# Where an adaLN modulation vector is summed while TensorE feeds sixteen state-space scans: on GpSimd, or in quarters of TensorE's columns

## The chip, the cores and the metric

The kernel runs on one core of a Trainium2 chip. The metric is the device time of one execution in microseconds (us). Its engines are TensorE (PE in the profile; its weight loads are PEld), VectorE (DVE), ScalarE (ACT), GpSimd (POOL) and SyncE (SP), whose queue issues nearly all transfers. Each engine works through its own instructions in order and waits for the others by semaphores.

## The reference, cut to what matters

One layer of a hybrid diffusion backbone, for 2048 tokens of 1024 channels and 256 context tokens, all in float32:

```python
sh1, sc1, gt1, sh2, sc2, gt2 = adaln(c, w_ada, b_ada)       # silu(c) @ w_ada + b_ada, six vectors of 1024
h = rms_norm(x, g_pre_mix) * (1 + sc1) + sh1                # the context likewise
u, xr, gr = split(h @ w_in, [512, 1024])                    # 512 channels each
y_s5  = s5_glu(D * u + S5 scans of u in both directions)    # 32 groups of 16 channels, 64 complex states each
y_lru = (RG-LRU of conv(xr) in both directions) * gelu(gr)
x = x + gt1 * rms_norm(concat(y_s5, y_lru) @ w_out, g_post_mix)
x = x + gt2 * rms_norm(swiglu(rms_norm(x, g_pre_ffn) * (1 + sc2) + sh2), g_post_ffn)
```

The change concerns the vectors gt1, sh2 and sc2 (numbers i = 2, 3, 4 of `w_ada`'s six blocks of 1024 columns). Each is a product of a row of 1024 numbers with a 1024x1024 block of `w_ada`. The first two vectors are made earlier, the last one (gt2) later; neither way is changed.

## The kernel before, in words

Products are in float32 precision on TensorE: a factor is split into a high and a low part (L59 on ScalarE rounds, L62 on VectorE takes the difference), and three matmuls (L70 to L72) make one product. A product of the input projection is one tile of 128 output channels for one block of 512 tokens: 8 slices of the 1024 inputs, three matmuls each, 24 in all. There are 12 tiles of channels: 0 to 3 are u for the S5 scans, 4 to 7 are the LRU input (stored in `XRD`), 8 to 11 the gate (stored in `GGD`). There are five token blocks, the context (n = 0, 256 tokens, no gate) and four of the latents.

**`u_pass`** makes tiles 0 to 5 (0 to 3 and the LRU input's first two) for all five blocks, normalising and transposing the tokens as it goes. **`rest_pass`** makes what is left, block 4 first, whose tokens still lie in SBUF, then blocks 0, 1, 2, 3, whose normalised tokens it loads again from `HD` (tile `hty`) and splits again into tiles `ht` and `wx`. It is a generator: each `next` issues one product ("a fill product" below) and returns what it is said to cost, 5.4 or 2.8.

**`s5_main`** handles 16 pairs of S5 groups. A half pair is one direction of one pair: TensorE makes the scan's inputs `pv` (a state group, L774: four matmuls with 64 output columns each), VectorE turns them, scans them and turns them back (L780 to L797, into `sf`). After the second direction of a pair TensorE reads out the pair before (a readout, L805 and L812: ten matmuls into the PSUM banks `py0` and `py1`), ScalarE applies GELU (`yt`, L814), and eight transfers store it in `YD`.

**`mix`** sets TensorE's order by hand for this stage. First it issues `AHEAD` fill products. Then `run` steps `s5_main`, adds `S5_FILL` to what is owed at each half pair, and issues fill products until what they are said to cost has paid it. At every half pair it also steps **`ada_s5`** once. What is left of the fills stands at the stage's end; then the LRU stage begins, whose convolution needs `XRD`.

`ada_s5` makes gt1, sh2 and sc2. `ada_sum` loads 128 rows of `w_ada` at a time (eight loads of 512 KB for a vector, through the two buffers `alw`); GpSimd multiplies each row by its number of silu(c) (L1128, L1130) and adds it to an accumulator `g` or `alacc` (L1131). What remains is a sum over the 128 partitions: `ada_row` takes it by a matmul with ones and spreads it over all partitions (L1143), adds a bias and multiplies by a gain on VectorE (L1144, L1145); `ada_col` takes it as columns, by eight matmuls with one column of ones (L1152). Both write into the readout's bank `py0`.

Of the kernel before, what the change touches and what calls it, by code (L numbers as in the profile page):

```python
# [9 lines left out]
F32 = mybir.dt.float32  # L10
F32R = mybir.dt.float32r
I32 = mybir.dt.int32
AF = mybir.ActivationFunctionType
ALU = mybir.AluOpType
MUL, ADD, SUB = ALU.mult, ALU.add, ALU.subtract
# [3 lines left out]
D = 1024  # L19
KT = 8  # L20
# [25 lines left out]
class Hybrid:  # L46
# [100 lines left out]
        self.ffn()  # L147


    AHEAD = 2  # L150
    S5_FILL, CONV_FILL, DECAY_FILL, GATES_FILL = 3.9, 0.1, 2.0, (0, 2, 2, 2)
    VW = 5
    XB = 5
    NPRE = 3
# [29 lines left out]
    def mix(self):  # L184


        def run(gen, fill, each=None):
            owed = 0.0
            for want in gen:
                if each:  # L190
                    next(each, None)
                owed += want
                while owed > 0:
                    owed -= next(fill, 1e9)

        aes, bes, self.wes = ExitStack(), ExitStack(), ExitStack()
        lru = self.lru(aes, bes)

        def first():
            yield from self.rest  # L200
            self.ies.close()

        with ExitStack() as es:
            ada = self.ada_s5(es)
            fill = first()
            for _ in range(self.AHEAD):
                next(fill)

            with self.tc.manual_schedule(engines={self.nc.tensor.engine}):
                run(self.s5_main(es), fill, ada)  # L210
            for g in (ada, fill):
                for _ in g:
                    pass
            next(lru)

        def rest():
            with ExitStack() as es:
                yield from self.glu(es)
            with ExitStack() as es:
                yield from self.out_s5(es)  # L220

        fill = rest()
        self.mm = (run, lru, fill, aes, bes)
# [122 lines left out]
    def u_pass(self, es):  # L346

        nc, A = self.nc, self.A
# [3 lines left out]
        def load(n):  # L352
            if n == 0:
                xt = [whole(8 + i) for i in range(2)]
                src = A["ctx"][0].rearrange("(j t) d -> t j d", t=T)
                for t in range(T):
                    nc.sync.dma_start(xt[t // 4][32 * (t % 4):32 * (t % 4) + 32, :], src[t])
                return [(xt[i], i * 128) for i in range(2)]
            tiles = []
            src = A["x"][0].rearrange("(b p t) d -> b p t d", b=2, t=T)  # L360
            for b in range(2):
                for i in range(2):
                    xt = xp.tile([128, D], F32, name="xt")
                    nc.sync.dma_start(xt, src[b, :, 2 * n - 2 + i, :])
                    tiles.append((xt, i * 256 + b * 128))
            return tiles

        def norm(tiles, junk):
            nt = len(tiles)
            ss = sp.tile([128, 4], F32, name="ss")  # L370
            rs = sp.tile([128, 4], F32, name="rs")
            for i, (x, _) in enumerate(tiles):
                self.square(junk, x, ss[:, i:i + 1])
            self.rstd(sp, rs[:, :nt], ss[:, :nt], nt, f"u{nt}")
            for i, (x, _) in enumerate(tiles):
                nc.scalar.activation(x, x, AF.Copy, scale=rs[:, i:i + 1])
# [47 lines left out]
        ws = self.load_w_in(0, self.wip, lambda: next(stages))  # L424
# [10 lines left out]
        for n in range(5):  # L435
            nxt, nh = None, []
            if n < 4:
                nxt = load(n + 1)
                norm(nxt, xp.tile([128, D], mybir.dt.bfloat16, name="junk", bufs=1))


            def after(i):
                if nxt and i in (22, 26, 30, 34, 40, 41, 42, 43):
                    turn(n + 1, nxt, nh, (len(nh),))

            for m in range(6):
                if (n, m) == (4, 2):

                    place = [(self.ht(40 + 2 * i), self.ht(41 + 2 * i)) for i in range(2)]
                    self.wrest = self.load_w_in(768, None, raw, place)  # L450
                product(n, m, hts, after)
                yield 5.2
            hts = nh or hts
        self.hts = hts
        self.wrest += self.load_w_in(1024, self.wip, raw)
        xes.close()
        es.close()
# [377 lines left out]
    def rest_pass(self, es):  # L835

        nc = self.nc
        st = self.pool(es, "ist", 2)
        ps = self.pool(es, "ips", 2, space=PSUM)
        MORE = 4  # L840
        places = cycle([lambda i=i: self.wx(i) for i in range(MORE)] + [lambda i=i: self.ht(i) for i in range(32, 40)])

        def fetch(n, k):
            ntok = 512 if n else CTX
            ht = next(places)()
            y = st.tile([128, 512], F32, name="hty", bufs=4)
            nc.sync.dma_start(y[:, :ntok], self.HD[n][k][:, :ntok])
            self.split(ht[:, 0, :ntok], ht[:, 1, :ntok], y[:, :ntok])
            return ht


        hts = self.hts
        for n, after in ((4, 0), (0, 1), (1, 2), (2, 3), (3, None)):
            ntok = 512 if n else CTX
            nxt = []

            def more(upto):
                if after is not None:
                    nxt.extend(fetch(after, k) for k in range(len(nxt), upto))

            for i in range(6 if n else 2):
                more(min(MORE, i + 1 if n else 2 * i + 2))
                pu = ps.tile([128, 512], F32, name="pu")
                wh, wl = self.wrest[i]
                for k in range(KT):
                    self.mm3(pu[:, :ntok], wh[:, k, :], wl[:, k, :], hts[k][:, 0, :ntok], hts[k][:, 1, :ntok],
                             k == 0, k == KT - 1)
                self.end_rest(n, i + 2, pu, st.tile([128, 512], F32, name="iev"))
                yield 5.4 if n else 2.8
            more(KT)  # L870
            hts = nxt
# [248 lines left out]
    def ada_sum(self, i, acc, tile):  # L1120

        nc, A = self.nc, self.A
        for k in range(KT):
# [7 lines left out]
                nc.gpsimd.tensor_tensor(acc, acc, w, op=ADD)  # L1131
            yield

    def ada_row(self, g, i, gi, rows, bank):

        nc = self.nc
        gain, bias = rows(), rows()
        nc.sync.dma_start(gain, self.A["norm_gains"][0, gi:gi + 1, :].to_broadcast([128, D]))
        nc.sync.dma_start(bias, self.A["b_ada"][:, i * D:(i + 1) * D].to_broadcast([128, D]))
        for h in range(2):  # L1140
            cs = slice(h * 512, (h + 1) * 512)
            pa = bank()
            nc.tensor.matmul(pa, self.ones, g[:, cs], start=True, stop=True)  # L1143
            nc.vector.tensor_tensor(g[:, cs], bias[:, cs], pa, op=ADD)  # L1144
            nc.vector.tensor_tensor(g[:, cs], gain[:, cs], g[:, cs], op=MUL)  # L1145

    def ada_col(self, i, acc, bank):

# [11 lines left out]
            v.scalar_tensor_tensor(self.A2, self.A2, 1.0, self.colsA[:, C_G + 16:C_G + 24], op0=ADD, op1=MUL)  # L1160

    def ada_s5(self, es):
        wp = self.pool(es, "alw", 2, side="right")
        tile = lambda: wp.tile([128, D], F32, name="alw")
        bank = lambda: self.psy.tile([128, 512], F32, name="py0")
        yield from self.ada_sum(2, self.g1, tile)
        for i in (3, 4):
            acc = wp.tile([128, D], F32, name="alacc", bufs=1)
            for k, _ in enumerate(self.ada_sum(i, acc, tile)):
                if k == 2 and i == 3:  # L1170
                    self.ada_row(self.g1, 2, 1, tile, bank)
                yield
            yield
            self.ada_col(i, acc, bank)

# [413 lines left out]
```

## Time and profile before

| | |
|---|---|
| median of 3 runs | 2322.15 us (2320.1 to 2322.33) |
| the profiled execution | 2329.66 us, of which the profile's span is 2327.9 us |
| PE busy | 2101.6 us (90%) |
| DVE busy | 1714.1 us (74%) |
| ACT busy | 994.3 us (43%) |
| POOL busy | 808.7 us (35%) |
| DMA | 403.29 MB, 173 GB/s over the span |

The stages follow one another: setup and `u_pass` to about 285 us, the S5 scans with the fill products to 566 us, then the LRU and the gated output of S5 to about 840 us, then the FFN. A row of the profile names the line, the engine, the operation, the tile written and the tiles read, how often it occurs, its time, and in brackets how long the engine sat idle before it and what it waited for. The matmuls of float32 operands that aren't split show as two records each. Every time of the profile is that of one execution.

### The profile page before, as it was taken

What the parts mean: (1) busy time and instruction counts of PE and PEld (TensorE: products, weight loads), DVE (VectorE), ACT (ScalarE), POOL (GpSimd) and SP (SyncE); (2) the same over time, 40 slices, a digit from 0 to 9 for tenths busy, and PEclk for the clock granted to TensorE, in tenths of its full rate; (3) what the DMA queues carried; (4) which work ended last, traced back from release to release, by engine and by line L of the source; (5) the groups of instructions that cost most, each with busy time, mean ns of one, the idle gap of its engine ahead of it and who ended that gap; (6) DMA issues with size and microseconds to landing.
All of it is one profiled execution on the core that took longest, in us unless ns stands there. A gap on an engine that the chain in (4) does not pass through costs nothing. (4 is left out here: it accounts for less than half of the span.)

```text
span 2327.9 us, 27391 instructions
## 1 busy us (share of the span) xinstructions
PE 2101.6 (90%) x9460; PEld 1662.1 (71%) x9460; DVE 1714.1 (74%) x2243; ACT 994.3 (43%) x1561; POOL 808.7 (35%) x478
## 2 busy tenths in 40 slices
PE   6599998897674899879999999999999999999987
PEld 1477865575564677658888887788888878888866
DVE  6985458999998748956777878977787763534768
ACT  4688412112777626763333334333333333232424
POOL 1431420440000003343335545656565511400682
PEclk8799999898886899889999999999999999999999
DMA  9577756765233377863443334544444375634663
GB/s 261 171 243 255 232 149 211 212 206 171 71 122 115 127 236 251 285 222 108 146 136 127 109 100 141 176 139 160 143 156 145 136 262 172 214 100 157 226 219 121
DMA packets 311627, 403.29 MB, mean 173 GB/s; under 512 B 60176, under 2 KB 222528, under 8 KB 309952
## 3 DMA queue, kind: packets, MB, share of 16 engines
q1 hardware_dynamic: 311360, 401.50, 53.2%
q8 instruction: 75, 1.23, 0.2%
q14 instruction: 64, 0.52, 0.1%
q0 software_dynamic: 128, 0.04, 0.0%
HBM read 269.33 MB, written 132.12 MB: 172 GB/s over the span
## 5 line engine op out<-in xcount | busy, mean ns | idle before, releaser
L70 PE MATMUL fp<-op,fws 128*128 128x512 f32 x1232 | 486.9, 396 | 8.2 <-ACT op L59 7.5
L71 PE MATMUL fp<-op,fws 128*128 128x512 f32 x1232 | 486.4, 395 | 3.6 <-DVE op L62 2.4
L72 PE MATMUL fp<-op,fws 128*128 128x512 f32 x1232 | 485.3, 394 | 0.0
L70 PEld LDWEIGHTS fp<-op,fws 128*128 128x128 f32 x1232 | 233.7, 190 | 62.5 <-ACT op L59 9.1
L71 PEld LDWEIGHTS fp<-op,fws 128*128 128x128 f32 x1232 | 233.0, 189 | 58.9 <-DVE op L62 5.0
L72 PEld LDWEIGHTS fp<-op,fws 128*128 128x128 f32 x1232 | 233.1, 189 | 51.8
L1029 PE MATMUL po<-gw,ga 128*128 128x512 f32 x616 | 241.7, 394 | 9.4 <-DVE gw L62 9.4
L1028 PE MATMUL po<-gw,ga 128*128 128x512 f32 x616 | 241.6, 394 | 4.1 <-ACT ga L59 2.8
L1030 PE MATMUL po<-gw,ga 128*128 128x512 f32 x616 | 237.8, 391 | 1.5 <-DVE ga L62 1.5
L1348 POOL TENSOR_TENSOR fs<-fraw 128x512 f32<-128x512 f32 x44 | 68.4, 1554 | 484.0 <-DMA fraw<-in_w_ffn_in_dram 381.6
L62 DVE TENSOR_TENSOR fws<-fraw,fws 128x512 fp32r<-128x512 f32 x132 | 126.7, 961 | 56.5 <-ACT fws L59 55.6
L59 ACT ACTIVATE fws<-fraw 128x512 fp32r<-128x512 f32 x132 | 82.9, 629 | 147.0 <-PE fp L72 79.2
L1029 PEld LDWEIGHTS po<-gw,ga 128*128 128x128 f32 x616 | 117.2, 190 | 34.5 <-DVE gw L62 10.1
L1028 PEld LDWEIGHTS po<-gw,ga 128*128 128x128 f32 x616 | 117.3, 190 | 29.3 <-ACT ga L59 3.2
L1030 PEld LDWEIGHTS po<-gw,ga 128*128 128x128 f32 x616 | 116.2, 189 | 26.7 <-DVE ga L62 2.4
L62 DVE TENSOR_TENSOR fws<-fs,fws 128x512 fp32r<-128x512 f32 x132 | 118.1, 895 | 8.1 <-ACT fws L59 6.3
L59 ACT ACTIVATE fws<-fs 128x512 fp32r<-128x512 f32 x132 | 82.5, 626 | 93.2 <-PE fp L72 92.2
L62 DVE TENSOR_TENSOR ga<-gys,ga 128x1024 fp32r<-128x1024 f32 (+2 forms) x88 | 113.8, 1299 | 10.8 <-ACT ga L59 10.8
L71 PE MATMUL pu<-ht,winh 128*128 128x512 f32 (+1 forms) x256 | 100.8, 394 | 10.9 <-DVE ht L62 10.9
L70 PE MATMUL pu<-ht,winh 128*128 128x512 f32 (+1 forms) x256 | 102.3, 404 | 6.7 <-ACT ut L416 3.4
L62 DVE TENSOR_TENSOR gw<-gch,gw 128x512 fp32r<-128x512 f32 x44 | 51.6, 1172 | 71.5 <-ACT gw L59 71.5
L62 DVE TENSOR_TENSOR gw<-graw,gw 128x512 fp32r<-128x512 f32 x44 | 37.1, 843 | 88.7 <-ACT gw L59 85.4
(532 smaller groups left out, 4751.3 us busy)
## 6 DMA issues: line engine op xcount, KB each, us to landing
fraw<-in_w_ffn_in_dram SPq DMA_DIRECT2D x88, 512.0 KB, 4.4
graw<-in_w_ffn_out_dram SPq DMA_DIRECT2D x99, 256.0 KB, 3.6
gys<-S SPq DMA_DIRECT2D x44, 512.0 KB, 4.0
A<-faf SPq DMA_DIRECT2D x33, 512.0 KB, 2.6
S<-ost SPq DMA_DIRECT2D x33, 512.0 KB, 3.0
alw<-in_w_ada_dram SPq DMA_DIRECT2D x24, 512.0 KB, 5.0
ost<-A SPq DMA_DIRECT2D x22, 512.0 KB, 5.1
gys<-A SPq DMA_DIRECT2D x22, 512.0 KB, 5.0
```

Of the source, the lines that this page charges most:

```text
L59: self.nc.scalar.activation(hi, src, AF.Identity)
L62: (eng or self.nc.vector).tensor_tensor(lo, src, hi.bitcast(F32), op=SUB)
L70: mm(ps, wh, xh, start=first, stop=False)
L71: mm(ps, wh, xl, start=False, stop=False)
L72: mm(ps, wl, xh, start=False, stop=last)
L1028: mm(ps, xh, wh, start=first, stop=False)
L1029: mm(ps, xh, wl, start=False, stop=False)
L1030: mm(ps, xl, wh, start=False, stop=last)
L1348: g.tensor_tensor(s[0], a21, a22, op=ADD)
```

## The change

In the kernel's words:

- `ada_sum` on GpSimd is replaced in `ada_s5` by `ada_half` on TensorE. It takes half a vector (512 columns): eight loads of 128x512 (256 KB each, eight buffers), and three steps later eight matmuls. Their left factor `alcz` has 32 columns, of which the first holds silu(c) and the others zeros; slice k of the 1024 rows goes to quarter k % 4 of TensorE's columns, that is to 32 of the 128 partitions of bank `py0`, and k + 4 is added there. ScalarE copies the bank to `g1` or `alacc`. Six of these replace 24 multiplications and 21 additions on GpSimd; the sum over the partitions (`ada_row`, `ada_col`) stays.
- `AHEAD` goes (it was 2), and `S5_FILL` rises from 3.9 to 4.5.
- For the last token block `u_pass` makes tiles 0 to 3 alone; the two LRU tiles of that block join `rest_pass`, which begins with them.
- `ada_row` loads its gain and bias in halves of 512. It is called for gt2 in the FFN too.

```diff
-    AHEAD = 2
-    S5_FILL, CONV_FILL, DECAY_FILL, GATES_FILL = 3.9, 0.1, 2.0, (0, 2, 2, 2)
+    S5_FILL, CONV_FILL, DECAY_FILL, GATES_FILL = 4.5, 0.1, 2.0, (0, 2, 2, 2)
...
             fill = first()
-            for _ in range(self.AHEAD):
-                next(fill)
...
-            for m in range(6):
+            for m in range(6 if n < 4 else 4):
...
         self.hts = hts
+        self.wrest = ws[4:] + self.wrest
         self.wrest += self.load_w_in(1024, self.wip, raw)
...
-            for i in range(6 if n else 2):
-                more(min(MORE, i + 1 if n else 2 * i + 2))
+            for m in range(0 if n == 4 else 2, 8 if n else 4):
+                if m >= 2:
+                    more(min(MORE, m - 1 if n else 2 * m - 2))
                 pu = ps.tile([128, 512], F32, name="pu")
-                wh, wl = self.wrest[i]
+                wh, wl = self.wrest[m]
...
+    def ada_half(self, i, h, acc, tile, cz, bank):
...
+        nc = self.nc
+        ws = []
+        for k in range(KT):
+            ws.append(tile())
+            nc.sync.dma_start(ws[k], self.A["w_ada"][0, k * 128:(k + 1) * 128, i * D + h * 512:i * D + (h + 1) * 512])
+        for _ in range(3):
+            yield
+        pa = bank()
+        for k in range(KT):
+            q = k % 4 * 32
+            nc.tensor.matmul(pa[q:q + 32, :], cz[:, k, :], ws[k], start=k < 4, stop=k >= 4)
+        nc.scalar.activation(acc[:, h * 512:(h + 1) * 512], pa, AF.Copy)
+        yield
...
     def ada_s5(self, es):
-        wp = self.pool(es, "alw", 2, side="right")
-        tile = lambda: wp.tile([128, D], F32, name="alw")
+        wp = self.pool(es, "alw", 1, side="right")
+        tile = lambda: wp.tile([128, 512], F32, name="alw", bufs=8)
...
-        yield from self.ada_sum(2, self.g1, tile)
-        for i in (3, 4):
-            acc = wp.tile([128, D], F32, name="alacc", bufs=1)
-            for k, _ in enumerate(self.ada_sum(i, acc, tile)):
-                if k == 2 and i == 3:
-                    self.ada_row(self.g1, 2, 1, tile, bank)
-                yield
+        cz = wp.tile([128, KT, 32], F32, name="alcz")
+        self.nc.gpsimd.memset(cz, 0.0)
+        self.nc.scalar.activation(cz[:, :, 0], self.cs[:, :, 0], AF.Copy)
+        for i in (2, 3, 4):
+            acc = self.g1 if i == 2 else wp.tile([128, D], F32, name="alacc")
+            for h in range(2):
+                yield from self.ada_half(i, h, acc, tile, cz, bank)
             yield
-            self.ada_col(i, acc, bank)
+            if i == 2:
+                self.ada_row(acc, 2, 1, tile, bank)
+            else:
+                self.ada_col(i, acc, bank)
```

TensorE's order at the start of the scans, before: the last product of tiles 0 to 3 (`pu_2665`), the two LRU tiles of `u_pass` (`pu_2693`, `pu_2722`), and the fill products from `pu_2794` on; `pv` are the state groups of the first pair, one matmul of the first drawn ahead. Only the first row of each 24 is shown.

```order
L774 MATMUL pv_2888<-u_2871,pe_2880 64x288
L70 MATMUL pu_2693<-ht8_2402,wx0_565 128x512
...
L70 MATMUL pu_2722<-ht8_2402,wx2_567 128x512
...
L774 MATMUL pv_2888<-u_2871,pe_2880 64x288 x3
L70 MATMUL pu_2794<-ht8_2402,ht4_2625 128x512
...
L70 MATMUL pu_2828<-ht8_2402,ht6_2627 128x512
...
L70 MATMUL pu_2937<-ht8_2402,winh0_2751 128x512
...
L774 MATMUL pv_2965<-u_2871,pe_2880 64x288 x4
```

The same place in the changed kernel, from the first state group on; here `pu_2665` is the last product of `u_pass`.

```order
L772 MATMUL pv_2756<-u_2739,pe_2748 64x288
L70 MATMUL pu_2665<-ht8_2402,winh3_475 128x512
...
L772 MATMUL pv_2756<-u_2739,pe_2748 64x288 x3
L70 MATMUL pu_2822<-ht8_2402,wx0_565 128x512
...
L772 MATMUL pv_2851<-u_2739,pe_2748 64x288 x4
L70 MATMUL pu_2872<-ht8_2402,wx2_567 128x512
...
L772 MATMUL pv_2901<-u_2777,pe_2786 64x288 x4
L70 MATMUL pu_2944<-ht8_2402,ht4_2625 128x512
```

Where five products stood between the first state group and the second, one stands now.

A sum on TensorE in the changed kernel, behind the readout of the first pair: the readout's last two matmuls, the eight quarters, and the next fill product.

```order
L810 MATMUL py0_2995<-sf1_2867,pc_2750 128x256
L810 MATMUL py1_2996<-sf1_2867,pc_2750 128x256
L1146 MATMUL py0_3017<-alw_2800,alcz_2797 32x512
L1146 MATMUL py0_3017<-alw_2802,alcz_2797 32x512
L1146 MATMUL py0_3017<-alw_2804,alcz_2797 32x512
L1146 MATMUL py0_3017<-alw_2806,alcz_2797 32x512
L1146 MATMUL py0_3017<-alw_2808,alcz_2797 32x512
L1146 MATMUL py0_3017<-alw_2810,alcz_2797 32x512
L1146 MATMUL py0_3017<-alw_2812,alcz_2797 32x512
L1146 MATMUL py0_3017<-alw_2814,alcz_2797 32x512
L70 MATMUL pu_3032<-ht8_2402,ht6_2627 128x512
```

The eight matmuls are new; the second sum of six (behind the readout of the third pair) and the last two (behind those of the tenth and twelfth) stand in the same way behind a readout, the third and fourth behind a state group.

The end of the stage on TensorE, before: the last fill product (its last matmul), a state group, and the readouts of the last two pairs (their first matmuls), then the next stage.

```order
L72 MATMUL pu_5047<-ht11_4618,winl3_2770 128x512
L774 MATMUL pv_5075<-u_4937,pe_4946 64x288 x4
L805 MATMUL py0_5097<-u_4788,md_4801 128x256
...
L805 MATMUL py0_5125<-u_4937,md_4950 128x256
...
L70 MATMUL pgl_5468<-gyh_5291,wgh0_5273 128x256
```

And in the changed kernel, from the readout of the last pair but one:

```order
L810 MATMUL py1_5140<-sf1_5040,pc_4840 128x256
L70 MATMUL pu_5161<-wx0_4243,winh3_2711 128x512
...
L72 MATMUL pu_5161<-ht11_4774,winl3_2712 128x512
L803 MATMUL py0_5195<-u_4979,md_4992 128x256
...
L70 MATMUL pgl_5538<-gyh_5361,wgh0_5343 128x256
```

The last fill product now stands behind the last state group and the readout of the last pair but one, with one readout behind it in place of a state group and two readouts.

## Rows read from the trace of the kernel before

**Rows 1.** Stage windows: length, busy us of each engine, PEclk (share of full clock), DMA.
```profile
285.50:566.00 280.50, 254.78 (x1285) 181.70 (x1284) 233.69 (x377) 53.20 (x107) 68.07 (x40) 0.94 0.64 189
566.00:840.00 274.00, 184.19 (x882) 153.69 (x883) 232.88 (x199) 179.03 (x204) 2.37 (x15) 0.81 0.37 124
```

**Rows 2.** PE's waits, 285.5 to 566 us: total us, times, longest.
```profile
PE py L1152 <- ACT yt L814: 7.5, 1, 7.5
PE pu L70 <- ACT wx L59: 7.1, 1, 7.1
PE pu L70 <- ACT iev L341: 3.3, 1, 3.3
...
PE py L805 <- ACT yt L814: 0.5, 1, 0.5
```

**Rows 3.** Timeline of PE, a fill product's first matmul and what follows: start, duration.
```profile
431.59 0.50 PE L70 MATMUL pu<-ht,ht 128*128 128x512 f32 x1
...
437.27 1.19 PE L774 MATMUL pv<-u,pe 128*64 128x288 f32 x8
```

**Rows 4.** Timeline of PE, a readout and a state group between fill products.
```profile
336.94 1.13 PE L805 MATMUL py<-u,md 128*128 128x256 f32 x4
338.00 2.00 PE L812 MATMUL py<-sf,pc 64*128 64x256 f32 x16
339.93 1.19 PE L774 MATMUL pv<-u,pe 128*64 128x288 f32 x8
341.05 0.50 PE L70 MATMUL pu<-ht,winh 128*128 128x512 f32 x1
```

**Rows 5.** Timeline of PE, the second half of the row sum.
```profile
397.98 1.12 PE L1143 MATMUL py<-g,ones 128*128 128x512 f32 x2 [1.06 <-DVE g L1144]
```

**Rows 6.** Timeline of PE, the first column sum with what follows it, and the second.
```profile
459.49 3.54 PE L1152 MATMUL py<-ones,alacc 128*128 128x1 f32 x16 [7.54 <-ACT yt L814]
462.96 2.19 PE L774 MATMUL pv<-u,pe 128*64 128x288 f32 x8
...
521.77 1.95 PE L1152 MATMUL py<-ones,alacc 128*128 128x1 f32 x16
```

**Rows 7.** Timeline of ACT ahead of the first column sum.
```profile
457.67 1.41 ACT L59 ACTIVATE wx<-hty 128x512 fp32r<-128x512 f32 x2 [12.00 <-DMA hty<-HD]
```

**Rows 8.** Window around it, columns as in the stage windows.
```profile
450.00:475.00 25.00, 17.46 (x82) 12.69 (x84) 23.39 (x38) 2.40 (x5) 6.39 (x5) 0.67 0.84 259
```

**Rows 9.** Timeline of DVE, two half pairs begin.
```profile
518.06 0.75 DVE L780 TENSOR_TENSOR ta<-pv,tab 128x576 f32<-128x576 f32 x1
...
523.69 0.75 DVE L780 TENSOR_TENSOR ta<-pv,tab 128x576 f32<-128x576 f32 x1
```

**Rows 10.** DVE's longest wait of the stage: total us, times, longest.
```profile
DVE ta L780 <- PE pv L774: 29.9, 10, 10.8
```

**Rows 11.** One line on DVE in the stage: duration ns minimum, median, maximum.
```profile
L793 DVE TENSOR_TENSOR xa<-zz,tab x32: 678/693/2714, 303.0 to 563.0; 128x512 f32<-128x512 f32 x32
```

**Rows 12.** Timeline of PE in the setup, two products with a two-column left factor.
```profile
59.84 1.88 PE L285 MATMUL vr<-wada,cs 128*2 128x512 f32 x4
```

**Rows 13.** Timeline of PE at the end of the stage.
```profile
557.98 1.19 PE L774 MATMUL pv<-u,pe 128*64 128x288 f32 x8
...
563.69 2.29 PE L812 MATMUL py<-sf,pc 64*128 64x256 f32 x16
577.71 0.80 PE L70 MATMUL pgl<-gyh,wgh 128*128 128x256 f32 x2 [11.74 <-ACT gyh L59]
578.92 1.65 PE L70 MATMUL pg<-xh,lwh 128*128 128x512 f32 x3 [0.41 <-ACT xh L59]
```

**Rows 14.** Timeline of SP at the end of the stage.
```profile
558.76 0.32 SPq L333 DMA_DIRECT2D GGD<-iev  x1
559.13 0.42 SPq L909 DMA_DIRECT2D xs<-XRD  x1
```

**Rows 15.** Timeline of DVE at the start of the next stage.
```profile
567.00 1.48 DVE L921 TENSOR_SCALAR xc<-xs,colsB 128x2307 f32<-128x2307 f32 x1
```

More of the change, by code (lines that the diff above doesn't have):

```diff
@@ L867, in rest_pass @@
                              k == 0, k == KT - 1)
-                self.end_rest(n, i + 2, pu, st.tile([128, 512], F32, name="iev"))
+                self.end_rest(n, m, pu, st.tile([128, 512], F32, name="iev"))
                 yield 5.4 if n else 2.8
@@ L1132, in ada_sum @@
             yield
+    def ada_half(self, i, h, acc, tile, cz, bank):
[12 more added lines that the diff above has]
+        yield
     def ada_row(self, g, i, gi, rows, bank):
         nc = self.nc
-        gain, bias = rows(), rows()
-        nc.sync.dma_start(gain, self.A["norm_gains"][0, gi:gi + 1, :].to_broadcast([128, D]))
-        nc.sync.dma_start(bias, self.A["b_ada"][:, i * D:(i + 1) * D].to_broadcast([128, D]))
         for h in range(2):
             cs = slice(h * 512, (h + 1) * 512)
+            gain, bias = rows()[:, :512], rows()[:, :512]
+            nc.sync.dma_start(gain, self.A["norm_gains"][0, gi:gi + 1, cs].to_broadcast([128, 512]))
+            nc.sync.dma_start(bias, self.A["b_ada"][:, i * D + h * 512:i * D + (h + 1) * 512].to_broadcast([128, 512]))
             pa = bank()
             nc.tensor.matmul(pa, self.ones, g[:, cs], start=True, stop=True)
-            nc.vector.tensor_tensor(g[:, cs], bias[:, cs], pa, op=ADD)
-            nc.vector.tensor_tensor(g[:, cs], gain[:, cs], g[:, cs], op=MUL)
+            nc.vector.tensor_tensor(g[:, cs], bias, pa, op=ADD)
+            nc.vector.tensor_tensor(g[:, cs], gain, g[:, cs], op=MUL)
     def ada_col(self, i, acc, bank):
```

## The prediction

> **What bounds the kernel now.** I first read the windows by stage, since the share of busy time over the whole span mixes stages with different limits. The stage of the S5 scans is 280.5 us long [rows 1], and nearly all of the change lies in it. TensorE is busy for 254.8 us of it, VectorE for 233.7, GpSimd for 68.1. VectorE's need is smaller than its busy time: an undisturbed half pair takes 523.69 - 518.06 = 5.63 us [rows 9], so the 32 half pairs need 180 us, and one operation that takes 0.69 us in the median takes up to 2.71 us [rows 11], in stretches where GpSimd sums. VectorE waits 29.9 us for state groups in ten places [rows 10]. So TensorE bounds the stage, and the second view is what TensorE does there.
>
> Its work, by count from the code and duration from the timeline: a fill product takes 437.27 - 431.59 = 5.68 us [rows 3]; a state group 341.05 - 339.93 = 1.12, a readout 339.93 - 336.94 = 2.99 [rows 4]; a half of the row sum 1.12 [rows 5]; a column sum 1.95 at full clock [rows 6]. From 285.5 on, before, there are two products of `u_pass` and 24 fill products (26 x 5.68 = 147.7), two products with 256 tokens, at half each (5.7), 32 state groups (35.8), 16 readouts (47.8), two halves of the row sum (2.2) and two column sums (3.9): **243.1 us**. The chain of waits of TensorE has ten kinds in the stage, from 7.5 us to 0.5, in sum **25.8 us** [rows 2]. What is left, 280.5 - 243.1 - 25.8 = **11.6 us**, is slower work and gaps: behind the wait of 7.5 us the column sum took 3.54 us in place of 1.95 and the state group 2.19 [rows 6], in a window whose granted clock is 0.67 [rows 8], that is, part of it went at 1.2 GHz in place of 2.4. Waits cost twice here.
>
> Third, the join to the next stage. TensorE ends the scans at 563.69 + 2.29 = 565.98, but the next stage does not hang on that: its convolution starts at 567.00 on VectorE [rows 15], behind a load of `XRD` issued at 559.13, which stands on SP's queue behind the store of the last fill product's result (558.76) [rows 14]. That product ended at 557.98 [rows 13]. The other chain, from the last readout through `YD`, lets TensorE start at 577.71, the convolution's at 578.92 [rows 13]; so the convolution's is later, by 1.2 us, and it counts from the *last fill product*, 8.0 us ahead of the last readout's end. The next stage has VectorE busy for 232.9 of 274 us [rows 1], so a shift of its start is passed on to the end.
>
> **The change part by part.** *Fill and `u_pass`.* The products are the same 26 and two halves behind 285.5; only their places move. The first half pair can be scanned behind one product in place of five, which takes away VectorE's early wait, not work of TensorE. Cost 0 on TensorE.
>
> *Six sums on TensorE.* No row shows a left factor of 32 columns. The nearest is that with two columns and 512 streamed: four records in 1.88 us [rows 12], 0.47 each, one behind the other. A sum is eight matmuls, 16 records: 7.5 us if they run singly. How far matmuls on parts of the array run beside each other is shown by halves: the state group (8 records, 288 streamed, 64 output columns) would be 8 x 0.47 x 288/512 = 2.1 us singly and takes 1.12; the readout's second part (16 records, 256 streamed, 64 input rows) would be 3.8 and takes 1.93 [rows 4]. Both go two at a time, with little lost. By quarters it would be 7.5/4 = 1.9; I take 2.0 per sum, **12 us** in all. The bounds are 1.9 and 7.5 (11 to 45 in all), with 3.9 (halves only) between. The copy by ScalarE lies beside a fill product except where `py0` is wanted next, which I count with the waits.
>
> The Trainium skill speaks for a worse price: its page "TensorE: Matmul & The Clock Gate", section "Packing small matmuls — row/col tiling", measures 2.38 times for three column tiles with 32 columns and 512 streamed. By it a sum would take 7.5/2.38 = 3.2 us, an estimate, and the six 7 us more than I count. The rows of halves come to 1.9 of 2 possible, better than that page's 2.38 of 3; no row here shows quarters.
>
> *GpSimd and the loads.* GpSimd's sums go, and with them VectorE's stretched operations. On a stage that TensorE bounds this buys cover, no time. 24 loads of 512 KB become 48 of 256 KB: the same bytes; with the row sum's, 26 more issues of about 0.4 us [rows 14] on SP's queue, some 10 us of 280, in bursts of eight. Behind a burst stand the pair's own loads and those of `hty`; the next half's burst waits until the last sum has freed its buffers. I take 0, since loads run pairs ahead; the upper bound is in the rival on stalls. For gt2 in the FFN two more issues: 0.8 us on SP, hidden.
>
> *Waits.* Of the 25.8: the 7.5 us came from ScalarE, whose GELU, which frees the bank `py0`, stood behind two splits of `wx` that had waited 12.0 us for `hty` [rows 7]. In the new order that column sum stands elsewhere; I take 0.8 for each of the two (1.6). The 3.3 for `iev` came where fill products stood one behind the other without state groups between; it goes. The 7.1 for `wx` is the entry into the next token block, whose tiles are loaded again; I take 5, since more products of the block ahead stand in front of it only by two. Four sums and the readouts behind them want a bank that ScalarE has just read, 0.5 each by the last of [rows 2] (2.0); the row sum keeps about 2.2 (1.06 of it in [rows 5]); the last readout 0.5. The waits on VectorE's `sf` (3.2 in two kinds) go with GpSimd's disturbance. Sum **11.3 us**. The slower work and gaps I scale with them: 11.6 x 11.3/25.8 = **5.1 us**.
>
> *The sum.* 243.1 + 12 + 11.3 + 5.1 = 271.5 us, 9.0 less than 280.5. But the end moves too: the last fill product now has one readout behind it (3.0 us) in place of a state group and two readouts (8.0), so it comes 5.0 us later within the stage. The convolution's chain therefore gains 9.0 - 5.0 = **4.0 us**; that from the last readout gains more and is not last. Against its own time of 2329.66 the profiled execution would give 2325.7; the median of the runs shown is 7.5 lower, 2322.15 - 4.0 = 2318.15. I predict **2318 us**. What a measurement of this kernel can tell from no change is about 0.2%, 4.6 us, so this is just below what can be told.
>
> **The rivals.**
>
> *The sums don't run four at a time.* For it: nothing here shows quarters; against: halves go at 0.53 and 0.51 of single. From 2.0 + 4.0/6 = 2.7 us per sum the whole is slower than before. Halves only: 6 x 1.9 = 11.4 more, 2329.5; singly: 33 more, 2351. The page named above would make it 2325.
>
> *The stall behind ScalarE or SP moves to a sum.* A sum wants `py0` behind a GELU; in the new order, too, there are readouts whose GELU stands behind splits that wait for `hty`, and those wait behind bursts of eight loads. One stall like that of 7.5 us [rows 2, 7] costs 7.5 and its slow clock (7.5 x 11.6/25.8 = 3.4): 10.9, or 2329. It decides from 14.1 us of waits on, 2.8 more than I count. So this is the rival on the other side that I hold likeliest.
>
> *The waits nearly vanish.* With scans ahead from the start and VectorE undisturbed TensorE may never wait: waits of 3 us and 1.4 of slow work leave 259.5, 21 less, 16 on the convolution's chain: 2306. For it: VectorE then needs about 200 of 260 us. Against: 7.1 of the waits are for reloaded tokens, which no part of the change makes earlier.
>
> *The change buys nothing, since TensorE bounds the stage and gets 12 us more.* This is the forecast's sum with waits of 14.1; it lies between the forecast and the second rival, at 2322.
>
> **How the numbers follow.** The forecast (2311 to 2323) 0.50; waits vanish (2300 to 2311) 0.16; sums dearer (2323 to 2351) 0.14; a stall moves (2320 to 2333) 0.20. The range leaves out the lower part of the second and the upper part of the third and fourth: 2306 to 2331. Faster by over 0.2% (under 2317.5): not quite half of the forecast's and all of the second, 0.41. Within 0.2%: the rest of the forecast's, 0.25, and 0.1 of the last two, 0.34. Slower: 0.25.
>
> **What would show it.** In the changed kernel's profile a sum (16 records into `py`) takes 2.0 us from its first to the next fill product; about 4 would mean halves. TensorE's waits of the stage sum to about 11, with no `iev` among them and the largest at the entry into a token block. VectorE's `xa` has no row near 2.7. The last fill product ends about 554, the last readout about 557, and the convolution starts at 563; GpSimd has next to nothing in the stage. The prediction is wrong if the waits' sum is above 14 or below 6, if a sum takes over 2.7 us, or if the convolution's start follows the last readout and not the last fill product.

## The result, and the profile after

The changed kernel takes 2333.11 us in the median of 4 runs (2329.96 to 2338.11), the kernel before 2321.77 us (2320.1 to 2322.33): a ratio of 1.0057, 95% interval 1.0044 to 1.0069. It is **11 us slower**, where 4 us faster was forecast. The two profiled executions differ by less, 2331.0 against 2327.9 us of span, since that of the kernel before lost some 8 us net in the FFN, far from the change (one tenth of the records of the FFN's second product took 55 us there, 43 in the changed kernel's).

The stage of the scans in the changed kernel, window by window; columns as in [rows 1]. The second row is the stretch around the first column sum, the third that behind the second.

```profile
285.50:566.00 280.50, 261.36 (x1362) 182.17 (x1361) 200.85 (x377) 54.90 (x110) 1.03 (x6) 0.95 0.64 191
436.00:460.00 24.00, 15.27 (x72) 11.73 (x72) 12.23 (x24) 3.93 (x8) 0.00 (x0) 0.72 0.80 258
529.00:539.00 10.00, 9.86 (x48) 7.91 (x48) 2.63 (x7) 0.96 (x3) 0.00 (x0) 0.83 0.56 150
```

GpSimd is out of the stage, and VectorE's busy time falls from 233.7 to 200.9 us. TensorE's waits, in answer to [rows 2]:

```profile
PE py L1168 <- ACT yt L812: 9.2, 2, 8.7
PE py L1159 <- ACT yt L812: 5.8, 1, 5.8
PE py L1159 <- DVE g L1160: 1.7, 1, 1.7
PE py L1146 <- ACT yt L812: 1.4, 3, 0.5
```

The waits for `iev` and for VectorE's `sf` are gone, as forecast, and so is the wait for `wx` of 7.1 us, of which 5 were expected to stay. In their place TensorE waits 8.7 us ahead of the first column sum (L1168) and 5.8 + 1.7 us at the row sum (L1159). The timeline of TensorE at the row sum, at the first column sum, at a sum of quarters and at the second column sum:

```profile
365.13 2.08 PE L1159 MATMUL py<-g,ones 128*128 128x512 f32 x2 [5.83 <-ACT yt L812]
368.93 2.07 PE L1159 MATMUL py<-g,ones 128*128 128x512 f32 x2 [1.72 <-DVE g L1160]
...
447.68 3.58 PE L1168 MATMUL py<-ones,alacc 128*128 128x1 f32 x16 [8.73 <-ACT yt L812]
...
480.23 1.92 PE L1146 MATMUL py<-alw,alcz 128*32 128x512 f32 x16 [0.47 <-ACT yt L812]
482.08 0.50 PE L70 MATMUL pu<-ht,winh 128*128 128x512 f32 x1
...
529.14 1.98 PE L1168 MATMUL py<-ones,alacc 128*128 128x1 f32 x16 [0.47 <-ACT yt L812]
```

A sum takes 482.08 - 480.23 = 1.85 us, and all six do. What ScalarE did ahead of the two long waits, and what stood on SP's queue ahead of the second:

```profile
361.88 1.93 ACT L59 ACTIVATE ht<-hty 128x512 fp32r<-128x512 f32 x3 [6.00 <-DMA hty<-HD]
...
364.71 0.64 ACT L812 ACTIVATE yt<-py 128x256 f32<-128x256 f32 x2
...
444.71 2.64 ACT L59 ACTIVATE wx<-hty 128x512 fp32r<-128x512 f32 x4 [10.32 <-DMA hty<-HD]
447.26 0.64 ACT L812 ACTIVATE yt<-py 128x256 f32<-128x256 f32 x2
```

```profile
432.44 5.42 SPq L1140 DMA_DIRECT2D alw<-in_w_ada_dram  x8
438.21 2.57 SPq L845 DMA_DIRECT2D hty<-HD  x4
```

The reader can follow it backwards: the column sum wants the bank `py0`; the GELU `yt` that empties it started at 447.26; ahead of it on ScalarE stand four splits, which waited 10.3 us for reloaded tokens `hty`; their four loads were issued from 438.21 on, behind a group of eight loads for a sum. It is the chain of [rows 7], now at two places: ScalarE waits 10.3 and 6.0 us there where it waited 12.0, and TensorE 8.7 and 5.8 us where it waited 7.5.

The end of the stage on TensorE, SP and VectorE, in answer to [rows 13 to 15]:

```profile
565.61 1.03 PE L803 MATMUL py<-u,md 128*128 128x256 f32 x4
566.57 2.00 PE L810 MATMUL py<-sf,pc 64*128 64x256 f32 x16
```

```profile
566.94 0.36 SPq L330 DMA_DIRECT2D GGD<-iev  x1
567.34 0.74 SPq L908 DMA_DIRECT2D xs<-XRD  x1
```

```profile
575.89 1.48 DVE L920 TENSOR_SCALAR xc<-xs,colsB 128x2307 f32<-128x2307 f32 x1 [0.59 <-DMA xs<-XRD]
```

The last readout ends 2.6 us later than before (568.57 against 565.98), the last fill product about 7.7 later (565.8 against 558.1), and the convolution 8.9 later.

**Accounts of the stage.** For each profiled kernel below: the stage from the end of the last product of tiles 0 to 3 to the end of the last readout, the work (243.1 us as in the prediction, and with the sums on TensorE 6 x 1.85 = 11.1 more; a sum takes 3.57 us in `sums_twice` and 1.00 in `half_sums`), TensorE's idle times of over 0.3 us, and what is left (slower work and small gaps). "Changed" stands for the changed kernel. Stage, work, waits and rest are those of the one profiled execution, the time is the median of the runs.

| kernel | stage | work | waits | rest | time, us | against before |
|---|---|---|---|---|---|---|
| before | 280.5 | 243.1 | 25.7 | 11.7 | 2321.8 | |
| changed | 283.0 | 254.2 | 18.7 | 10.1 | 2333.1 | 1.0057 |
| order_alone | 264.9 | 243.1 | 14.7 | 7.1 | 2308.8 | 0.9945 |
| sums_alone | 284.1 | 254.2 | 21.9 | 8.0 | 2331.2 | 1.0037 |
| late_sums | 272.7 | 254.2 | 14.1 | 4.4 | 2326.1 | 1.0028 |
| loads_other_queue | 276.7 | 254.2 | 14.7 | 7.8 | 2329.5 | 1.0026 |
| sums_twice | 285.7 | 264.5 | 12.5 | 8.7 | 2337.9 | 1.0061 |
| half_sums | 278.6 | 249.1 | 21.4 | 8.1 | 2330.0 | 1.0036 |
| one_load | 262.1 | 254.2 | 6.1 | 1.8 | 2312.8 | 0.9962 |

### The profile page after: what moved, and what is told of

It reads as the page before. It is cut to its first block, busy times and chain, and to the rows that moved or that the text cites. A ratio compares the mean times of both kernels' runs of the same rounds, so it can differ in the third digit from the quotient of the medians.

```text
span 2331.0 us, 27574 instructions
## 1 busy us (share of the span) xinstructions
PE 2111.9 (91%) x9556; PEld 1663.2 (71%) x9556; DVE 1671.7 (72%) x2243; ACT 998.5 (43%) x1568; POOL 724.5 (31%) x434
## 4 chain that ended last, share of the span: by engine, by line
PE 58%; DVE 11%; ACT 4%; DMA 4%; issue 3%; POOL 1%; SPq 0%; DVEq 0%; ACTq 0%; POOLq 0%
PE fp L70 12%; PE fp L71 12%; PE fp L72 12%; PE po L1027 4%; PE po L1028 4%; PE po L1029 4%; DVE lt L945 1%; PE pu L70 1%; DVE xc L922 1%; DVE gy L1549 1%; PE pu L71 1%; PE pu L72 1%; PE fpg L1029 1%; PE fpg L1027 1%; PE fpg L1028 1%
## 5 line engine op out<-in xcount | busy, mean ns | idle before, releaser
L62 DVE TENSOR_TENSOR fws<-fraw,fws 128x512 fp32r<-128x512 f32 x132 | 128.4, 974 | 58.6 <-ACT fws L59 57.7
L71 PE MATMUL pu<-ht,winh 128*128 128x512 f32 (+1 forms) x256 | 99.3, 388 | 10.3 <-DVE ht L62 10.3
L72 PE MATMUL pu<-ht,winl 128*128 128x512 f32 (+1 forms) x256 | 98.0, 383 | 0.0
L59 ACT ACTIVATE ga<-gys 128x1024 fp32r<-128x1024 f32 (+2 forms) x88 | 82.6, 941 | 32.9 <-DMA gys<-A 20.7
```

What stands on the lines that cost most here:

```text
L59: self.nc.scalar.activation(hi, src, AF.Identity)
L62: (eng or self.nc.vector).tensor_tensor(lo, src, hi.bitcast(F32), op=SUB)
L71: mm(ps, wh, xl, start=False, stop=False)
L72: mm(ps, wl, xh, start=False, stop=last)
```

## The experiments

The kernel before ran beside each group of them, with medians of 2320.6 to 2323.4 us. A ratio is to those runs.

**Taken apart: the order, and the sums.** `order_alone` undoes the sums on TensorE (and the halves of the row sum's loads), `sums_alone` the rest:

```diff
# sums_alone, on the changed kernel (order_alone is the kernel before with the opposite)
+    AHEAD = 2
-    S5_FILL = 4.5 ...
+    S5_FILL = 3.9 ...
-            for m in range(6 if n < 4 else 4):
+            for m in range(6):
-        self.wrest = ws[4:] + self.wrest
...
```

> The new order alone: AHEAD gone, S5_FILL 4.5, the two LRU tiles of the last block in the fill; the sums stay on GpSimd with 512 KB loads. Theory: without eight loads in a burst ahead of the reloaded tokens the stalls are shorter, but the last fill product stands 5 us later within the stage; 2320 to 2328. Rival (the new order alone costs the time, the sums nothing): 2331 to 2335. Rival (the sums' work costs it): 2311 to 2318.

> The six sums on TensorE alone: AHEAD stays 2, S5_FILL 3.9, u_pass six products in the last block, as before the change. Theory (stalls and the late last fill product cost the time, the work of the sums is paid by VectorE's and GpSimd's relief): 2318 to 2327, with the last fill product 8 us ahead of the last readout's end, as before. Rival (the sums' 11 us on TensorE cost the time): 2331 or more.

Measured: the order alone 2308.8 us (0.9945, interval 0.9926 to 0.9965), the sums alone 2331.2 (1.0037, 1.0019 to 1.0054). The first lies below all three ranges given, the second is the rival's: **the order is worth 13 us, and the sums on TensorE cost 9 with the old order and 24 with the new one.** What TensorE waited for in the order alone:

```profile
PE py L1142 <- DVE g L1143: 7.0, 1, 7.0
PE py L1151 <- ACT yt L812: 6.4, 1, 6.4
```

Both sums stall here too, somewhat shorter, but the row sum now waits for VectorE between its halves and not for ScalarE. No other wait is over 0.7 us.

**Are the two stalls what costs?** `late_sums` has one more step ahead of the row sum and the column sums:

```diff
             yield
+            yield
             if i == 2:
                 self.ada_row(acc, 2, 1, tile, bank)
```

> The changed kernel, with one more step of the generator ahead of the row sum and of each column sum, so that a state group or a fill product stands between a readout and the sum that wants its bank. Theory (two stalls behind ScalarE's GELU, 5.8 and 8.7 us, with the half clock that follows them, cost the time): TensorE's waits in the stage fall from about 20 us to under 8, the last fill product ends some 14 us sooner than in the changed kernel (near 552), and the time falls to 2316 to 2322. Rival (the sums' own work on a TensorE that bounds the stage costs the time): the waits change, but the time stays within 4 us of 2333.

2326.1 us (1.0028, 1.0012 to 1.0044), 7 less than the changed kernel; the stage is 10.3 us shorter and the rest halves. But waits of 14.1 us stay, in new places: 5.1 between the halves of the row sum and 5.0 ahead of a sum of quarters, whose GELU stood behind the splits this time. The direction is the theory's, the size is about half of it.

**What does the sums' work cost?** `sums_twice` issues the eight matmuls again over the first, `half_sums` leaves out four of them (and so half of the rows), `one_quarter` puts all eight into one quarter of the columns:

```diff
-        for k in range(KT):
+        for k in [*range(KT), *range(KT)]:                  # sums_twice
...
+            nc.tensor.matmul(pa[0:32, :], cz[:, k, :], ws[k], start=k == 0, stop=k == KT - 1)   # one_quarter
```

> The changed kernel with the eight matmuls of each sum issued twice, the second time over the first, which adds 6 x 1.85 = 11.1 us of the same work at the same places, and no load. Theory (TensorE bounds the stage, so work put there passes to the time in full): 2340 to 2347. Rival (the sums lie beside waits that would be there anyway, and cost by their loads and places alone): 2331 to 2337.

> The changed kernel with four of the eight matmuls of each sum (the sums leave out half of their rows), and all loads: 6 x 0.9 = 5.4 us less of TensorE's work. Theory (work is taken up in part by the waits, as in the run of twice the matmuls): 2330 to 2334. Rival (work passes to the time in full): 2325 to 2329.

> The changed kernel with all eight matmuls of a sum in the first quarter of TensorE's columns, accumulated there, and the accumulator's other partitions set to zero by GpSimd. Theory (1.85 us for a sum is four quarters at a time): a sum takes 6.9 to 7.5 us, and six of them pass 30 us more to the time, 2360 to 2368. Rival (quarters don't run beside each other, a matmul with few columns is short by itself): a sum stays near 1.9 us and the time near 2333.

Against the kernel before beside it the changed kernel takes 11.3 us more. Twice: 2337.9 us (1.0061, 1.0039 to 1.0082), 14.5 more, for 6 x (3.57 - 1.85) = 10.3 us of added work. Half: 2330.0 (1.0036, 1.0022 to 1.0049), 8.7 more, for 6 x (1.85 - 1.00) = 5.1 us less. Both intervals overlap the changed kernel's, so neither difference can be told by itself. One quarter: 2346.0 (1.0095, 1.0075 to 1.0115), 22.6 more, which is clear, for a sum as in this row of its timeline:

```profile
342.93 7.05 PE L1145 MATMUL py<-alw,alcz 128*32 128x512 f32 x16 [0.47 <-ACT yt L812]
349.92 0.50 PE L70 MATMUL pu<-ht,winh 128*128 128x512 f32 x1
```

So 1.85 us is indeed four quarters at a time. But of the 6 x (6.98 - 1.85) = 30.8 us that one quarter adds, 11.3 reach the time. TensorE's waits shrink meanwhile, from 18.7 us in the changed kernel to 7.1 (and to 12.5 with twice the work). The theory that work on TensorE passes in full was too simple; the reading that fits is that the late tokens arrive while TensorE works.

**Are the loads what makes the tokens late?** `loads_other_queue` issues the sums' loads from GpSimd's queue; `loads_spread` issues three, three and two over the three steps; `late_spread` is that with late_sums; `one_load` loads for the first sum alone and multiplies the same tiles six times (wrong rows for five halves):

```diff
-            nc.sync.dma_start(ws[k], self.A["w_ada"] ...
+            nc.gpsimd.dma_start(ws[k], self.A["w_ada"] ...          # loads_other_queue
...
-        for _ in range(3):
-            yield
+            if k in (2, 5, 7):                                      # loads_spread
+                yield
...
+            ws.append(tile() if (i, h) == (2, 0) else self.ws0[k])  # one_load
+            if (i, h) == (2, 0):
+                nc.sync.dma_start(ws[k], ...
```

> The changed kernel with the sums' 48 loads of 256 KB issued by GpSimd's queue in place of SP's. Theory (the reloaded tokens come late because their loads stand on SP's queue behind a burst of eight): the waits of 5.8 us ahead of the row sum and of 8.7 us ahead of the first column sum shrink to under 3 each, and the time is 2318 to 2326. Rival (the loads are late because the transfers share the engines and the bandwidth, or because the tokens' buffers come free late): the waits stay, 2330 to 2336.

> The changed kernel with the eight loads of a sum issued three, three and two over the three steps ahead of it, in place of all at once. Theory (the reloaded tokens come late because 2 MB for a sum stand ahead of them on SP's queue and in the transfers): the waits ahead of the row sum and the first column sum (5.8 and 8.7 us) shrink to under 4 each, the last fill product ends 6 to 12 us sooner than 565.8, and the time is 2320 to 2327. Rival (the tokens are late because their own buffers come free late): the waits stay, 2330 to 2336.

> Both edits on the changed kernel: loads spread over three steps, and one more step ahead of the row sum and the column sums. Theory (late_sums kept waits of 5.1 and 5.0 us; spreading takes away the second): 2316 to 2323, about level with the kernel before, since the sums' 11.1 us of work stay. Rival (the sums cost nothing once the stalls are gone): 2306 to 2312, level with the order alone.

> The changed kernel with loads for the first half sum alone: the other five sums multiply the same eight tiles again, so that gt1's second half, sh2 and sc2 come from the wrong rows; matmuls and places stay. Theory (the loads make the reloaded tokens late): the waits of 5.8 us ahead of the row sum and 8.7 us ahead of the first column sum fall under 3 each, stage 283.0 to 268 to 273 us, time 2317 to 2323. Rival (the matmuls and their places do it): waits and time stay, 2329 to 2335.

The other queue takes the two waits from 5.8 and 8.7 to 4.1 and 5.3 us and some 4 us off the time (2329.5), between what the theory and the rival gave. Ahead of the first column sum the tokens' loads then had no group of loads ahead of them on SP's queue, but they were slower from there to the split:

```profile
429.33 2.84 SPq L845 DMA_DIRECT2D hty<-HD  x4
438.02 0.63 ACT L59 ACTIVATE wx<-hty 128x512 fp32r<-128x512 f32 x1 [6.09 <-DMA hty<-HD]
```

That is 8.7 us from the first issue to the first split, where the changed kernel takes 444.71 - 438.21 = 6.5. So the place on the queue goes, and a delay in the transfers stays. Spreading did not test what it was meant to: at the first column sum the eight loads still stood in one group ahead of `hty` on SP's queue, the waits were 5.0 and 7.8, and the time 2333.5; with late_sums 2328.0. `one_load` decides: **2312.8 us (0.9962, 0.9947 to 0.9977), 20 less than the changed kernel, with every matmul in its place**, and below the range of its theory. (Its row sum also loads gain and bias into buffers of their own.) Here are the longest waits left, the split that held up the first column sum (idle 3.4 us for the tokens in place of 10.3), and the median time from issue to landing of the tokens' loads (the last number of a row) in `one_load`, in the changed kernel, in the order alone and in `loads_other_queue`:

```profile
PE py L1162 <- DVE g L1163: 3.3, 1, 3.3
PE py L1148 <- ACT yt L812: 1.4, 3, 0.5
```

```profile
427.35 0.63 ACT L59 ACTIVATE wx<-hty 128x512 fp32r<-128x512 f32 x1 [3.37 <-DMA hty<-HD]
```

```profile
hty<-HD SPq DMA_DIRECT2D x24, 256.0 KB, 3.6
```

```profile
hty<-HD SPq DMA_DIRECT2D x24, 256.0 KB, 6.1
```

```profile
hty<-HD SPq DMA_DIRECT2D x24, 256.0 KB, 5.4
```

```profile
hty<-HD SPq DMA_DIRECT2D x24, 256.0 KB, 7.1
```

The order alone, at 2308.8 us, loads as many bytes for its sums, but otherwise: singly or in pairs of 512 KB, seven of the 24 loads ahead of the stage (from 246.9 us on), where the changed kernel issues all 48 in the stage (from 289.5 on) and mostly six to eight at a time. Whether the groups do it or the bytes within the stage, no run shows by itself.

**Two controls that turned out otherwise.** `gpsimd_halves` keeps the changed kernel's order and loads and does the sums on GpSimd in halves; `order_no_loads` is the order alone with GpSimd's sums over two tiles loaded once (wrong rows):

```diff
+            a, c = acc[:, h * 512:(h + 1) * 512], self.cs[:, k, 0:1]     # gpsimd_halves, behind each load
+            nc.gpsimd.tensor_scalar(ws[k], ws[k], c, 0.0, op0=MUL, op1=ADD)
+            nc.gpsimd.tensor_tensor(a, a, ws[k], op=ADD)
```

> The changed kernel's order and loads (halves of 256 KB in groups of eight), but the sums on GpSimd, eight multiplications and seven additions of 128x512 for a half; no matmul and no copy for them. Theory (loads and places cost about as much as the matmuls): stage 270 to 276 us, time 2317 to 2324, well above the 2308.8 of the order alone. Rival (the matmuls cost it all): stage 263 to 267, time 2306 to 2312.

> The order alone with loads of two tiles of w_ada in place of 24: GpSimd multiplies and adds the same two tiles again and again, so that gt1, sh2 and sc2 come from the wrong rows; its work stays. Control for one_load (2312.8 us, stage 262.1). Theory (without loads the matmuls of the sums pass to the time nearly in full, about 8 to 11 us): stage 250 to 255, time 2299 to 2305. Rival (GpSimd's sums cost VectorE as much as the matmuls cost TensorE): stage 259 to 264, time 2307 to 2314.

2329.9 and 2331.1 us, both near the changed kernel, but by waits of their own: for GpSimd's sum itself in the first, and in the second, where nothing paces GpSimd any more and its sums of gt1 and sh2 fall together from 294 to 356 us, for VectorE's scans. The first two rows are of `gpsimd_halves`, the others of `order_no_loads`:

```profile
PE py L1160 <- POOL alacc L1146: 11.2, 1, 11.2
PE py L1160 <- DVE g L1161: 7.0, 1, 7.0
```

```profile
PE py L810 <- DVE sf L794: 8.5, 4, 6.4
PE py L1143 <- DVE g L1144: 5.8, 1, 5.8
```

Neither separates loads from matmuls. The second says something else: GpSimd's sums beside the scans are not free once TensorE waits for VectorE, whose operation `xa` takes up to 2.71 us in that run and 0.69 in the median.

**The join to the next stage.** `fill_48` has S5_FILL 4.8 in the changed kernel, `order_39` 3.9 in the order alone:

> The changed kernel with S5_FILL 4.8 in place of 4.5, so that two state groups and two readouts stand behind the last fill product again (about 8 us in place of 3). Theory (the next stage hangs on the last fill product): its convolution starts 4 to 6 us sooner than in the changed kernel by the fill product's place alone, and the time is 2326 to 2330, with both stalls still there. Rival (the next stage hangs on the last readout): no change, 2331 to 2335.

> The order alone (sums on GpSimd, 2308.8 us) with S5_FILL 3.9 in place of 4.5. In the order two fill products then stand behind the last readout. Theory (the next stage hangs on the last fill product): the last fill product comes 11 us behind the last readout, the convolution waits for it, and the time is 2314 to 2322. Rival (the next stage hangs on the last readout): 2305 to 2311.

What was expected of `fill_48` was wrong by its sign: 2340.3 us. The last fill product came sooner (559.3) and the convolution 7.5 us sooner (568.4), but now it ran on VectorE between the parts of the last scan, and TensorE waited for that scan (and 6.9 us for reloaded tokens at another place):

```profile
PE py L810 <- DVE sf L794: 11.4, 2, 10.1
```

The last readout ended at 580.7 in place of 568.6, and the gated output, which hangs on it, started 10 us later. In `order_39` the last fill product ended at 559.6, 11.0 us behind the last readout, the convolution started at 566.9, 13.9 later than in the order alone, and the time is 2330.4, 21.5 more and above the 2322 that the theory allowed. So the next stage hangs on both ends, and the place of the last fill product is a balance: too late and the convolution waits, too early and it takes VectorE from the last scan.

**What of the order gains, and can it be bettered?** `ahead_0` is the kernel before with AHEAD 0; `two_banks` is the order alone with the two halves of the row sum in `py0` and `py1`; `order_spread` is that with three steps more ahead of each column sum:

> The kernel before with AHEAD 0 in place of 2, and nothing else: S5_FILL stays 3.9 and u_pass makes six products in the last block. Theory (the order alone gains 13 us because the scans start sooner and TensorE meets the reloaded tokens with other work between): two thirds of it, 2311 to 2316, unless the fill lags; in the order two fill products stand ahead of the last readout, so that the last fill product ends only 3 us ahead of it, in place of 8. Rival (what gains is S5_FILL 4.5 and the LRU tiles joined to the fill): 2320 to 2326.

> The order alone (2308.8 us) with the two halves of the row sum in the two readout banks, py0 and py1, and nothing else. Theory (the 7.0 us that TensorE waits between the halves is a wait for VectorE to empty the one bank): that wait goes, the stage is 256 to 260 us, the time 2300 to 2305. Rival (the stall moves to the reloaded tokens): a wait for wx or ht takes its place, 2306 to 2312.

> The new order with the sums on GpSimd (as in the run of the order alone, 2308.8 us), the two halves of the row sum in the two readout banks in place of one, and three steps more ahead of each column sum. Theory (what is left to gain there is TensorE's waits of 7.0 us for VectorE between the halves of the row sum and of 6.4 us for ScalarE ahead of the first column sum, with the half clock behind them): both waits go, the last readout comes 12 to 18 us sooner, the time is 2292 to 2300. Rival (with the new order VectorE and the loads bound the stage): other waits take their place, 2304 to 2311.

`ahead_0`: 2319.3 (0.9989, 0.9976 to 1.0001), no difference that can be told; so most of the 13 us needs the rest of the order, and which part of it wasn't tried. `two_banks`: 2316.0, above both ranges; the 7.0 us went, and the wait ahead of the first column sum grew from 6.4 to 12.6. `order_spread`: 2315.2; both waits went, and 7.2 us came for a state group behind VectorE. In both the stall moved. **The order alone, at 2308.8 us, is the fastest that was run, and beats both kernels.**

## Why the prediction was wrong

- **The sums' work** was priced at 2.0 us each; it took 1.85. That quarters run four at a time was right, and the estimate of 3.2 us by the Trainium skill (page "TensorE: Matmul & The Clock Gate", section "Packing small matmuls — row/col tiling") was too high for this case: 6.98 us from the first matmul to the next fill product in one quarter, against 1.85 in four, is 3.8 times.
- **The loads were costed at nothing, and this is the step that failed.** That the loads bring "the same bytes" was true of the kernel and not of the stage, into which seven loads of 512 KB moved from ahead of it. "I take 0, since loads run pairs ahead" held for the loads of the pairs, not for the reloaded tokens `hty`: ahead of the first column sum ScalarE stood idle for them from 434.4 us on (444.71 - 10.32), and they were issued at 438.21, behind eight loads for a sum. Without 40 of the sums' loads the time falls by 20 us and the stage to 262.1 us, below the 271.5 forecast. Both the place on SP's queue and slower transfers have a part: another queue takes away 4 of the 18.7 us of waits, while the tokens' landing takes 7.1 us there. How the rest divides is open.
- **The waits** were therefore mis-sized: 11.3 us forecast, 18.7 measured, and with them the slower work and gaps, 5.1 against 10.1. The single terms: column sums 1.6 against 9.2; row sum 2.2 against 7.5 (5.8 + 1.7); the entry into the next token block 5 against 0.5. The wait for the tokens did not shrink; it moved from the products to the sums, because the sums want a bank whose GELU stands behind the splits.
- **The second rival was what happened**, "the stall behind ScalarE or SP moves to a sum". It was priced for one stall, at 2329; there were two, at 2333. Its threshold of 14.1 us of waits was passed.
- **The order** was costed at 0 for its work, which is right, and its gain lay in the waits. Without the sums the prediction's own terms give 243.1 + 11.3 + 5.1 = 259.5 us of stage; the order alone shows 264.9. Had the two parts been forecast apart, the order would have been a gain.
- **The end of the stage** was right: 2.8 us from the last fill product to the last readout's end in place of 7.9 before, and the convolution follows the fill product. Its start is passed on, as was assumed: from there to the last gate matmul of the LRU it is 210 to 213 us in every profiled kernel but `fill_48` (226). That it takes VectorE from the last scan when it comes early was not seen.
- **GpSimd's relief** buys cover and no time, as said: VectorE's wait for state groups is 5.8 us in the order alone, with GpSimd beside it, and 57.7 in the changed kernel:

```profile
DVE ta L778 <- PE pv L772: 5.8, 3, 3.0
```

```profile
DVE ta L778 <- PE pv L772: 57.7, 18, 7.7
```

Of the 24.3 us between the order alone and the changed kernel the two profiles place 283.0 - 264.9 = 18.1 in the stage (11.1 work, 4.0 waits, 3.0 rest), and 3.0 in a later start of the stage, where the code is the same and executions differ by some 4. Another 3.3 lie at the other end: from the last gate matmul of the LRU to the first matmul on the LRU's output (`fpg`) it is 92.1 us before, 92.2 in the order alone, and 95.4 in the changed kernel. It is 94.9 or more in all ten profiled kernels with the whole sums on TensorE, whatever their order and loads, and at most 93.9 in the eight with the sums on GpSimd; in `half_sums` it is 92.2. Why is open.

## What to carry to other kernels

When work moves to another engine, price the transfers' new places first: ask which load is wanted soonest after its issue, and what will stand ahead of it. A wait on an in-order queue moves to whatever stands behind it; an operation that needs a buffer freed by a busy engine should stand where that engine has nothing late ahead of it. And when two edits come together, forecast them apart: here one gained 13 us and the other hid it.

## What was not expected of the hardware

- Matmuls with 32 output columns ran in four quarters beside each other nearly without loss: 16 records in 1.85 us against 6.98 in one quarter, and the second eight matmuls in `sums_twice` added 3.57 - 1.85 = 1.72.
- TensorE's clock fell behind the second column sum of the changed kernel after a wait of only 0.47 us: in the window from 529 to 539 the granted clock is 0.83 (0.50, that is 1.2 GHz, from 531 to 533), and the fill product behind took 7.2 us in place of 5.7. Ahead of the fall stood a state group, a readout, the wait and 16 records of one column each. In the kernel before, where a readout, a state group and the same 16 records stood without a wait, the fill product behind them ran at full clock (5.7 us). No run separates the wait from the narrow matmuls.
